# Early MLP units with a bank of their own for the third product, transposes at given places in PE's queue, two more pairs of split tiles, other banks for the first merge product

## The chip, the cores and the metric

The kernel runs on one core of one Trainium2 chip. A core has TensorE (PE in the profile; its weight loads are the row PEld), VectorE (DVE), ScalarE (ACT), GpSimd (POOL) and the queue SP, which here issues all DMAs. SBUF is the working memory; PSUM, eight banks of 128 x 512 float32, takes the results of PE. The metric is the device time of one execution in microseconds; less is better.

## The reference

One layer of a decoder trunk on x of 1024 tokens by 1024 channels, float32.

```python
h = rms_norm(x, norm_mix_pre)
proj = h @ w_in                       # q, k, v, z, ... of two mixers, two merge gates
y_a = gdn_branch(...)                 # gated DeltaNet, 4 heads
y_b = gla_branch(...)                 # gated linear attention, 4 heads
merged = sigmoid(gate_a) * (y_a @ w_out_a) + sigmoid(gate_b) * (y_b @ w_out_b)
x = x + rms_norm(merged @ w_o, norm_mix_post)
h = rms_norm(x, norm_mlp_pre)
u = square(relu(h @ w_mlp_up))        # 1024 -> 4096
x = x + rms_norm(u @ w_mlp_down, norm_mlp_post)
```

## The kernel before

**Precision and PE's work.** Each float32 product is made of three matmuls of a rounded format: an operand is split into a high part (cast by ACT) and the rest (subtraction by DVE). `split` makes such a pair in the pool `wsp`, tags `wh` and `wl`, three buffers each; `mm3` (line 256) issues hi*hi, hi*lo, lo*hi into one PSUM bank. A full matmul here is 128 x 128 weights by 512 columns.

**Queues.** The program is traced in the order of the code. A scheduler then gives each engine a fixed order: of what it takes to be ready at a modelled time, what comes first in the code goes first; `tc.high_priority(offset=...)` moves instructions forward (splits by `HP` = 2000 places, evictions of banks by `HPM` = 1500 or `HPE` = 2000). On the chip every engine then works its queue strictly in order and waits on semaphores. A tile of a tag with n buffers waits until a tile before it has had its last reader.

**PSUM.** The pool `psg` has four banks (`gbank()`, tile g), `psm` one bank each for the tags t, l, r, o (`mbank`, tiles mt, ml, mr, mo).

**Stages in order of time.** Input norm, projection and the two mixers; the merge; W_o with its norm and residual; MLP up; MLP down. The change touches the middle three:

1. *Merge* (lines 1002 to 1036). `load_o` loads and splits the outputs of the two mixers (`oaH/oaL`, `obH/obL`) through two `oraw` buffers. Gate groups 6 and 7 are computed: each a product into four g banks, a tanh of each bank into a tile `sg` (two buffers) and a store. Then, for c = 0 to 3, `ya` = four k tiles of branch A into four g banks (48 matmuls), `yb` = eight k tiles of branch B into four g banks (96 matmuls); DVE multiplies them with the gates and adds.

2. *W_o and norm* (lines 1100 to 1156). For each half u of the tokens: for two column halves c, sixteen steps in all, PE multiplies the merged activations of four token tiles (i = 0 to 3, one g bank each) by one k tile of w_o, twelve matmuls a step. The banks of each c are evicted into `m` (four tiles of that tag). Then for each token tile: the norm, the residual with a reloaded x (`xt`), the store of `d_x1`, the second norm by `stt(m, xt, rs, wpre2, ...)`, and a *turn*: eight PE transposes of `m` into the banks t and l, evicted into blocks. For u = 0 these are X11 and X21 (and their splits R11, R21); for u = 1, X12 and X22, and the sums that a Strassen-like scheme of seven products needs: T1, T2, R22, and X11, X21 rewritten. The X blocks are tiles of the tag `wu` of the pool `z`, which has four buffers. In the code each turn stands right behind its token tile's norm, ahead of the next half's products.

3. *MLP up.* A unit n (of 16) makes two blocks of 128 hidden channels (n and 16 + n), for both token halves, by seven products P1 to P7 of twelve matmuls each. For the first eight units (`NE` = 8), P1 and P2, which need only the first half of the tokens, run ahead (lines 1158 to 1180, "the P1/P2 loop", sixteen products in pairs of units), and their results go to DRAM (`d_p`, `d_u[0]`). `prep(n)` loads the weights of a unit (tag `wu`) and makes their sums (`ss`) on DVE. T3 and T4 are split from X22 and X21 behind the loop. Then, in a loop over n, an early unit (n < 8) runs P6 into bank A (r or o in turn), P5 into a g bank C, P7 added to A, P3 added to C, P4 added to A; each result is read out of A between the products and P1's saved result `p1` is added on DVE. A late unit runs P6, P5, P7, then P1 of the next unit, P4, P2 of the next unit, P3. `product` (line 1228) splits the operand in `wsp` and issues the twelve matmuls. `u_sums` makes the sums for the down projection and stores them; in the late units `down_sums` prepares sums of the down weights.

The lines of the products of a unit, before:

```python
s_P6(n); prep(n + 2); s_P5(n); s_P7(n)
# n >= 8: down_sums; and if a late unit follows: s_P1(n + 1), s_P4(n), s_P2(n + 1), s_P3(n)
# otherwise: s_P3(n); s_P4(n)
u_sums(n)
```

Of the kernel before, what the change touches and what calls it, by code (L numbers as in the profile page):

```python
# [7 lines left out]
F32 = mybir.dt.float32  # L8
# [3 lines left out]
ALU = mybir.AluOpType  # L12
# [11 lines left out]
TAU = 16.0  # L24
DFF = 4096
NE = 8
HP = 2000
HPX = 600
HPE = 2000
# [103 lines left out]
def kernel(  # L133
# [855 lines left out]
    with tc.tile_pool(name="mp", bufs=1, reuse_waits="tile") as mp:  # L989
        def load_o(src, n, nm):  # L990
            hi = mp.tile([P, n, S], F32R, name=nm + "H")
            lo = mp.tile([P, n, S], F32R, name=nm + "L")
            for k in range(n):
                for u in range(2):
                    us = slice(u * 512, u * 512 + 512)
                    raw = mp.tile([P, 512], F32, tag="oraw", name="oraw", bufs=2)
                    SP.dma_start(out=raw, in_=src[k, :, us])
                    with tc.high_priority(offset=HP):
                        A.copy(out=hi[:, k, us], in_=raw)
                        tt(lo[:, k, us], raw, hi[:, k, us].bitcast(F32), ALU.subtract)  # L1000
            return hi, lo
        oaH, oaL = load_o(d_oa, 4, "oa")
        obH, obL = load_o(d_ob, 8, "ob")
        run(gate_groups([int(c) for c in GTAIL.split()]))
        hp.release()
        bot = tc.alloc_tile_pool(name="bot", bufs=4, side="right", reuse_waits="tile")

        def big():
            return bot.tile([P, 8, 512], F32R, tag="big", name="big")

        mg_ = [(big(), big()) for _ in range(2)]
        for c in range(4):
            def sl(w):
                return lambda s: [w[:, 2 * s:2 * s + 2, c * 256:c * 256 + 256]]
            ya = gemm_fm(sl(woa), 4, oaH, oaL)
            ga = {}
            for b in range(2):
                for u in range(2):
                    sg = mp.tile([P, 512], F32, tag="sa", name="sa", bufs=4)
                    SP.dma_start(out=sg, in_=d_sig[c * 2 + b, :, u * 512:u * 512 + 512])  # L1020
                    with tc.high_priority(offset=HPE):
                        tt(sg, ya[b][u], sg, ALU.mult)
                    ga[b, u] = sg
            yb = gemm_fm(sl(wob), 8, obH, obL)
            for b in range(2):
                for u in range(2):
                    us = slice(u * 512, u * 512 + 512)
                    sg = mp.tile([P, 512], F32, tag="sb", name="sb", bufs=2)
                    SP.dma_start(out=sg, in_=d_sig[8 + c * 2 + b, :, us])
                    with tc.high_priority(offset=HPE):  # L1030
                        tt(sg, yb[b][u], sg, ALU.mult)
                    mg = ga[b, u]
                    with tc.high_priority(offset=HPM):
                        tt(mg, mg, sg, ALU.add)
                    A.copy(out=mg_[u][0][:, c * 2 + b, :], in_=mg)
                    tt(mg_[u][1][:, c * 2 + b, :], mg, mg_[u][0][:, c * 2 + b, :].bitcast(F32), ALU.subtract)
# [52 lines left out]
    with tc.tile_pool(name="op", bufs=1, reuse_waits="tile") as op:  # L1089
# [7 lines left out]
            tt(blk[:, kl, cs], src, blk[:, ks, cs].bitcast(F32), ALU.subtract)  # L1097

        k4 = slice(0, 4)
        for u in range(2):  # L1100
            ms, s2s = [], []
            for i in range(4):
# [2 lines left out]
            for c in range(2):  # L1105
                banks = [gbank() for _ in range(4)]
                cs = slice(c * 512, c * 512 + 512)
                for kt in range(KT):
                    hi, lo = load_slab512(wov[:, kt, cs], wsp, "w")
                    for i in range(4):  # L1110
                        il = slice(i * P, i * P + P)
                        mm3(banks[i], mg_[u][0][:, kt, il], mg_[u][1][:, kt, il], hi, lo, kt == 0, kt == KT - 1)
                with tc.high_priority(offset=HPE):
                    for i in range(4):
                        jk = op.tile([P, 512], F32, tag="jk", name="jk", bufs=1)
                        act(jk, banks[i], AF.Square, accum_out=s2s[i][:, c:c + 1])
                        tt(ms[i][:, cs], banks[i], wpost[:, cs], ALU.mult)
            if u == 1:
                T2, T1 = big(), big()
            for i in range(4):  # L1120
                t = u * 4 + i
                tsl = slice(t * P, t * P + P)
                rs = op.tile([P, 1], F32, tag="rs", name="rs", bufs=3)
                tt(rs, s2s[i][:, 0:1], s2s[i][:, 1:2], ALU.add, eng=G)
                rsqrt(rs, rs, 1.0 / D, EPS)
                m = ms[i]
                xt = z.tile([P, D], F32, tag="ss", name="xt", bufs=2)
                SP.dma_start(out=xt, in_=x2[tsl, :])
                stt(xt, m, rs, xt, ALU.mult, ALU.add)
                SP.dma_start(out=d_x1[tsl, :], in_=xt)  # L1130
                rs = op.tile([P, 1], F32, tag="rs", name="rs", bufs=3)
                act(m, xt, AF.Square, accum_out=rs)
                rsqrt(rs, rs, 1.0 / D, EPS)
                stt(m, xt, rs, wpre2, ALU.mult, ALU.mult)
                il = slice(i * P, i * P + P)
                pv = []
                for g in range(2):
                    pt = mbank("tl"[g])
                    for k in range(4):
                        T.transpose(out=pt[:, k * P:(k + 1) * P], in_=m[:, (g * 4 + k) * P:(g * 4 + k + 1) * P],  # L1140
                                    identity=ident)
                    pv.append(pt.rearrange("p (k c) -> p k c", c=P))
                if u == 0:
                    for g, n in enumerate(("11", "21")):
                        A.copy(out=X[n][:, :, il], in_=pv[g])
                        hilo(R[n], k4, il, X[n][:, :, il])
                else:
                    x11, x21, x12, x22 = (X[n][:, :, il] for n in ("11", "21", "12", "22"))
                    A.copy(out=x12, in_=pv[0])
                    tt(x22, pv[1], x12, ALU.subtract)  # L1150
                    hilo(R["22"], k4, il, pv[1])
                    tt(x12, x12, x11, ALU.subtract)
                    tt(x11, x22, x11, ALU.add)
                    hilo(T2, k4, il, x11)
                    hilo(T1, k4, il, x12)
                    tt(x21, x21, x11, ALU.subtract)

        for n in range(0, NE, 2):
            pair = range(n, n + 2)
            bank = {}  # L1160
            for p, k0, blk in (("P1", 0, R["11"]), ("P2", 4, R["21"])):
                for m in pair:
# [6 lines left out]
                    for k in range(4):  # L1169
                        mm3(bank[m], hi[:, k, :], lo[:, k, :], blk[:, k, :], blk[:, 4 + k, :],  # L1170
                            p == "P1" and k == 0, k == 3, p == "P2")
                    e = op.tile([P, 512], F32, tag="e", name="e", bufs=3)
                    with tc.high_priority(offset=HPM):
                        if p == "P1":
# [49 lines left out]
    with tc.tile_pool(name="ml", bufs=1, reuse_waits="tile") as ml:  # L1224
        RT = dict(P1=R["11"], P2=R["21"], P3=R["22"], P4=T4, P5=T1, P6=T2, P7=T3)
        reserve(ml, (("ev", 512, 10), ("us", 512, 6)))

        def product(n, p, ps, first):
            hi, lo = split(un[n][p], [P, 4, P], wsp, "w")
            for k in range(4):  # L1230
                mm3(ps, hi[:, k, :], lo[:, k, :], RT[p][:, k, :], RT[p][:, 4 + k, :], first and k == 0, k == 3, not first)

# [24 lines left out]
        def store(b, n, t):  # L1257
            SP.dma_start(out=d_u[b][:, n, :], in_=t)  # L1258

        def from_A(n, out):  # L1260
            if n < NE:
                tt(out, un[n]["A"], un[n]["p1"], ALU.add)
            else:
                A.copy(out=out, in_=un[n]["A"])

        def s_P1(n):
            x = un[n]
            x["A"] = mbank("ro"[n % 2])
# [14 lines left out]

        def s_P6(n):
            x = un[n]
            if n < NE:
                x["A"] = mbank("ro"[n % 2])
            product(n, "P6", x["A"], n < NE)
            x["c12"] = ev("c12")
            with tc.high_priority(offset=HPM):  # L1290
                from_A(n, x["c12"])

        def s_P5(n):
            x = un[n]
# [3 lines left out]
        def s_P7(n):  # L1298
# [1 line left out]
            product(n, "P7", x["A"], False)  # L1300
            x["c22"] = ev("c22")
            with tc.high_priority(offset=HPM):
                from_A(n, x["c22"])
                tt(x["c22"], x["C"], x["c22"], ALU.add)
            relu2(x["c22"], x["c22"])
            store(2, n, x["c22"])
# [1 line left out]
        def s_P4(n):  # L1308
# [1 line left out]
            product(n, "P4", x["A"], False)  # L1310
            x["c21"] = ev("c21")
            with tc.high_priority(offset=HPM):
                if n < NE:
                    from_A(n, x["c21"])
                    act(x["c21"], x["c21"], AF.Relu)
                else:
                    act(x["c21"], x["A"], AF.Relu)
            act(x["c21"], x["c21"], AF.Square)
            store(1, n, x["c21"])

        def s_P3(n):
            x = un[n]
            product(n, "P3", x["C"], False)
            with tc.high_priority(offset=HPM):
                tt(x["c12"], x["C"], x["c12"], ALU.add)
            relu2(x["c12"], x["c12"])

        def u_sums(n):
# [14 lines left out]
        for n in range(NU):  # L1343
            if n + 1 < NE:
                again(n + 1)
            s_P6(n)
            if n + 2 < NU:
                prep(n + 2)
# [1 line left out]
            s_P7(n)  # L1350
            if n >= NU // 2:
                down_sums(2 * n - NU)
            if NE <= n + 1 < NU:
                s_P1(n + 1)
                s_P4(n)
                s_P2(n + 1)
# [136 lines left out]
```

## Time and profile before

| | |
|---|---|
| median of 3 runs | 1718.45 us (1717.08 to 1719.82) |
| the profiled execution | 1717.46 us, of which the span is 1715.8 us |
| granted TensorE clock, mean | 0.994 |
| PE busy | 1659.6 us (97%), 9174 matmuls |
| DVE, ACT, POOL busy | 987.4, 769.1, 135.5 us |
| P1/P2 loop | from 1069.40 to 1120.09 us: 50.69 us, PE busy 47.97 |
| early units | from 1120.09 to 1235.98 us: 115.89 us, PE busy 108.74 |
| late units, first down product | from 1235.98 to 1413.60 us: 177.62 us, PE busy 175.46 |

A row of the profile in order of time reads: start in us from the span's start, duration in us, engine, line of the code, operation, output tile <- input tiles, shapes, how many in a row, and in brackets the idle time before it and what ended it. A line of a helper (67 is the matmul, 71 the transpose, 165 the two-operand DVE pass, 236 the cast of a split) stands for all its callers, so the tile names tell where an instruction belongs. Matmuls overlap: in a full stream one begins every 0.23 us, though its row says 0.39. A row of the waits reads: engine, tile and line <- engine, tile and line waited for: total us, times, longest.

### The profile page before, as it was taken

How to read it: one execution, taken by the hardware profiler on the slowest of the kernel's cores; microseconds unless marked ns; L12 is line 12 of the kernel's file. 1: busy time of each engine (PE TensorE's matmuls, PEld its weight loads, DVE VectorE, ACT ScalarE, POOL GpSimd, SP SyncE). 2: the span in 40 equal slices, each digit the busy share in tenths (PEclk: the TensorE clock that was granted, in tenths of full speed). 3: DMA queues.
4: the chain of work that ended last, by engine and by line, in shares of the span. 5: the costliest groups of instructions: out<-in, count | busy, mean ns of one | idle time of the engine just before them, and what ended most of it. 6: DMA issues, size and time to landing. Idle time of an engine off the chain costs nothing. (4 is left out here: it accounts for less than half of the span.)

```text
span 1715.8 us, 24483 instructions
## 1 busy us (share of the span) xinstructions
PE 1659.6 (97%) x9174; PEld 1402.4 (82%) x9174; DVE 987.4 (58%) x1678; ACT 769.1 (45%) x1576; POOL 135.5 (8%) x222
## 2 busy tenths in 40 slices
PE   7999999999999999999999999989999999999997
PEld 6888778878898998998788887777787778888886
DVE  5677565872544436543444455967776665564764
ACT  5456545643533235433421245744455555443442
POOL 2010111111101000101100011100000000000021
PEclk9999999999999999999999999999999999999999
DMA  5222213322211211123633344766578798776763
GB/s 166 56 72 75 83 38 91 91 62 68 76 44 44 62 50 50 37 63 126 218 117 112 122 163 150 244 223 221 179 259 279 239 327 304 257 261 224 245 226 136
DMA packets 186405, 251.39 MB, mean 147 GB/s; under 512 B 23351, under 2 KB 108430, under 8 KB 186286
## 3 DMA queue, kind: packets, MB, share of 16 engines
q1 hardware_dynamic: 186286, 249.83, 45.3%
q8 instruction: 72, 1.18, 0.3%
q14 instruction: 47, 0.39, 0.1%
HBM read 185.79 MB, written 63.98 MB: 146 GB/s over the span
## 5 line engine op out<-in xcount | busy, mean ns | idle before, releaser
L165 DVE TENSOR_TENSOR wl<-w,wh 128x512 fp32r<-128x512 f32 x181 | 125.7, 694 | 231.7 <-ACT wh L236 229.8
L67 PE MATMUL g<-hT,wh 128*128 128x512 f32 (+1 forms) x600 | 239.3, 399 | 1.5 <-DVE gr L174 0.9
L67 PE MATMUL g<-hL,wh 128*128 128x512 f32 (+1 forms) x600 | 232.9, 388 | 0.0
L67 PE MATMUL g<-hT,wl 128*128 128x512 f32 (+1 forms) x600 | 232.1, 387 | 0.0
L236 ACT CAST wh<-w 128x512 fp32r<-128x512 f32 x184 | 113.9, 619 | 212.8 <-PE g L67 194.4
L67 PE MATMUL g<-wh,hT 128*128 128x256 f32 x640 | 185.6, 290 | 0.0
L67 PE MATMUL g<-wh,hL 128*128 128x256 f32 x640 | 182.1, 285 | 0.0
L67 PE MATMUL g<-wl,hT 128*128 128x256 f32 x640 | 182.0, 284 | 0.0
L67 PE MATMUL g<-big 128*128 128x512 f32 x768 | 176.7, 392 | 2.4 <-ACT big L1219 2.4
L67 PEld LDWEIGHTS g<-big 128*128 128x128 f32 x768 | 145.2, 189 | 33.1 <-ACT big L1219 2.8
L165 DVE TENSOR_TENSOR big<-ru,big 128x1024 fp32r<-128x1024 f32 x53 | 64.9, 1224 | 115.9 <-ACT big L1219 115.5
L67 PEld LDWEIGHTS g<-hT,wh 128*128 128x128 f32 x600 | 113.6, 190 | 21.9 <-ACT sg L177 1.3
L67 PEld LDWEIGHTS g<-hT,wl 128*128 128x128 f32 x600 | 113.5, 189 | 21.6 <-DVE wl L165 0.2
L67 PEld LDWEIGHTS g<-hL,wh 128*128 128x128 f32 x600 | 113.9, 190 | 18.7 <-issue 1.0
L1219 ACT CAST big<-ru 128x1024 fp32r<-128x1024 f32 x53 | 55.8, 1053 | 154.8 <-PE g L67 57.7
L67 PEld LDWEIGHTS g<-wh,hT 128*128 128x128 f32 x640 | 123.1, 192 | 1.4 <-issue 1.0
L67 PEld LDWEIGHTS g<-wl,hT 128*128 128x128 f32 x640 | 123.2, 193 | 1.2 <-issue 1.0
L67 PEld LDWEIGHTS g<-wh,hL 128*128 128x128 f32 x640 | 123.2, 193 | 0.1
L177 ACT ACTIVATE c<-c 128x512 f32<-128x512 f32 x104 | 64.9, 631 | 49.6 <-DVE c L165 46.8
L67 PE MATMUL g<-wh,big 128*128 128x512 f32 x256 | 80.4, 392 | 0.0
L67 PE MATMUL mr<-big,wh 128*128 128x512 f32 x192 | 61.2, 400 | 6.1 <-DVE c L165 3.3
L165 DVE TENSOR_TENSOR big<-rv,big 128x1024 fp32r<-128x1024 f32 x53 | 64.5, 1218 | 0.1
(418 smaller groups left out, 3394.7 us busy)
## 6 DMA issues: line engine op xcount, KB each, us to landing
ru<-d_u SPq DMA_DIRECT2D x53, 512.0 KB, 4.5
w<-in_w_in_dram SPq DMA_DIRECT2D x80, 256.0 KB, 2.7
rv<-in_w_mlp_down_dram SPq DMA_DIRECT2D x37, 512.0 KB, 5.3
wu<-in_w_mlp_up_dram SPq DMA_DIRECT2D x32, 512.0 KB, 5.3
d_u<-c SPq DMA_DIRECT2D x56, 256.0 KB, 3.7
d_u<-us SPq DMA_DIRECT2D x48, 256.0 KB, 2.5
us<-in_w_mlp_down_dram SPq DMA_DIRECT2D x48, 256.0 KB, 4.2
xt<-in_x_dram SPq DMA_DIRECT2D x16, 512.0 KB, 5.4
```

Source lines behind the costliest of these rows:

```text
L67: return self.eng.matmul(out, lhsT, rhs, start=start, stop=stop, skip_group_check=more)
L165: (eng or V).tensor_tensor(out=out, in0=a, in1=b, op=op)
L177: A.activation(out=out, in_=a, func=func, **kw)
L236: A.copy(out=hi, in_=raw)
L1219: A.copy(out=s4[:, i], in_=raw)
```

## The change

Four edits, in the order of the program:

- The first `ya` (c = 0) of the merge goes to the banks r, o, l, t instead of the four g banks.
- The turns leave their place behind the norms and become a function. `TURNS` gives their places: for the first token half, after the steps 2, 5, 6 and 9 of the sixteen steps of the second half's W_o product; for the second half, after the products 3, 6, 10 and 12 (counted from 0) of the sixteen of the P1/P2 loop.
- `product` puts the split pairs of the products 1 and 3 of every five into the pool `wraw` (four buffers, no longer used at that stage) instead of `wsp`, in early and late units.
- The early units run as `early(n)`: P6 into A; P7 into a g bank d of its own, with no add on PE; P5 into a g bank c; P4 added to d; P3 added to c. The saved `p1` is added once, to P6's result, and that sum is added to d's contents on DVE. For the last early unit P1 and P2 of unit 8 stand between. Late units keep their order.

```diff
+TURNS = (2, 5, 6, 9), (3, 6, 10, 12)
...
-            ya = gemm_fm(sl(woa), 4, oaH, oaL)
+            ya = gemm_fm(sl(woa), 4, oaH, oaL, banks=[[mbank("r"), mbank("o")], [mbank("l"), mbank("t")]] if c == 0 else None)
...
+        def turn(u, i):
+            m = msu[u][i]
...
+            if u == 0:
+                for g, n in enumerate(("11", "21")):
+                    A.copy(out=X[n][:, :, il], in_=pv[g])
+                    hilo(R[n], k4, il, X[n][:, :, il])
+            else:
+                x11, x21, x12, x22 = (X[n][:, :, il] for n in ("11", "21", "12", "22"))
+                A.copy(out=x12, in_=pv[0])
+                tt(x22, pv[1], x12, ALU.subtract)
+                hilo(R["22"], k4, il, pv[1])
+                tt(x12, x12, x11, ALU.subtract)
+                tt(x11, x22, x11, ALU.add)
+                hilo(T2, k4, il, x11)
+                hilo(T1, k4, il, x12)
+                tt(x21, x21, x11, ALU.subtract)
...
                         mm3(banks[i], mg_[u][0][:, kt, il], mg_[u][1][:, kt, il], hi, lo, kt == 0, kt == KT - 1)
+                    if u and c * KT + kt in TURNS[0]:
+                        turn(0, TURNS[0].index(c * KT + kt))
...
+                    step = 2 * n + (2 if p == "P2" else 0) + m - n
+                    if step in TURNS[1]:
+                        turn(1, TURNS[1].index(step))
...
         def product(n, p, ps, first):
-            hi, lo = split(un[n][p], [P, 4, P], wsp, "w")
+            if turns[0] % 5 in (1, 3):
+                hi, lo = (wraw.tile([P, 4, P], F32R, tag="w", name="w" + x) for x in "hl")
+                with tc.high_priority(offset=HP):
+                    A.copy(out=hi, in_=un[n][p])
+                    tt(lo, un[n][p], hi.bitcast(F32), ALU.subtract)
+            else:
+                hi, lo = split(un[n][p], [P, 4, P], wsp, "w")
+            turns[0] += 1
...
+        def early(n):
+            x = un[n]
+            a, c, d = mbank("ro"[n % 2]), gbank(), gbank()
+            x["c12"], x["c22"], x["c21"] = ev("c12"), ev("c22"), ev("c21")
+            product(n, "P6", a, True)
+            with tc.high_priority(offset=HPM):
+                tt(x["c12"], a, x["p1"], ALU.add)
+            product(n, "P7", d, True)
+            with tc.high_priority(offset=HPM):
+                tt(x["c22"], d, x["c12"], ALU.add)
+            if n + 2 < NU:
+                prep(n + 2)
+            product(n, "P5", c, True)
+            with tc.high_priority(offset=HPM):
+                tt(x["c22"], c, x["c22"], ALU.add)
+            product(n, "P4", d, False)
+            with tc.high_priority(offset=HPM):
+                tt(x["c21"], d, x["c12"], ALU.add)
+            relu2(x["c22"], x["c22"])
+            store(2, n, x["c22"])
+            if n + 1 == NE:
+                s_P1(n + 1)
+            product(n, "P3", c, False)
+            with tc.high_priority(offset=HPM):
+                tt(x["c12"], c, x["c12"], ALU.add)
+            relu2(x["c21"], x["c21"])
+            store(1, n, x["c21"])
+            if n + 1 == NE:
+                s_P2(n + 1)
+            relu2(x["c12"], x["c12"])
...
+            if n < NE:
+                early(n)
+                u_sums(n)
+                continue
```

More of the change, by code (lines that the diff above doesn't have):

```diff
@@ L1099 @@
         k4 = slice(0, 4)
+        msu = []
+        def turn(u, i):
+            m = msu[u][i]
+            il = slice(i * P, i * P + P)
+            pv = []
+            for g in range(2):
+                pt = mbank("tl"[g])
+                for k in range(4):
+                    T.transpose(out=pt[:, k * P:(k + 1) * P], in_=m[:, (g * 4 + k) * P:(g * 4 + k + 1) * P],
+                                identity=ident)
+                pv.append(pt.rearrange("p (k c) -> p k c", c=P))
+            if u == 0:
[12 more added lines that the diff above has]
+                tt(x21, x21, x11, ALU.subtract)
         for u in range(2):
@@ L1134 @@
                 stt(m, xt, rs, wpre2, ALU.mult, ALU.mult)
[L1135 to L1156, printed above, removed]
+            msu.append(ms)
         for n in range(0, NE, 2):
@@ L1226 @@
         reserve(ml, (("ev", 512, 10), ("us", 512, 6)))
+        turns = [0]
         def product(n, p, ps, first):
-            hi, lo = split(un[n][p], [P, 4, P], wsp, "w")
+            if turns[0] % 5 in (1, 3):
[6 more added lines that the diff above has]
+            turns[0] += 1
             for k in range(4):
@@ L1258, in store @@
             SP.dma_start(out=d_u[b][:, n, :], in_=t)
[L1260 to L1264, printed above, removed]
         def s_P1(n):
@@ L1285, in s_P6 @@
             x = un[n]
-            if n < NE:
-                x["A"] = mbank("ro"[n % 2])
-            product(n, "P6", x["A"], n < NE)
+            product(n, "P6", x["A"], False)
             x["c12"] = ev("c12")
             with tc.high_priority(offset=HPM):
-                from_A(n, x["c12"])
+                A.copy(out=x["c12"], in_=x["A"])
         def s_P5(n):
@@ L1302, in s_P7 @@
             with tc.high_priority(offset=HPM):
-                from_A(n, x["c22"])
+                A.copy(out=x["c22"], in_=x["A"])
                 tt(x["c22"], x["C"], x["c22"], ALU.add)
@@ L1312, in s_P4 @@
             with tc.high_priority(offset=HPM):
[L1313 to L1317, printed above, removed]
+                act(x["c21"], x["A"], AF.Relu)
             act(x["c21"], x["c21"], AF.Square)
@@ L1352 @@
                 down_sums(2 * n - NU)
-            if NE <= n + 1 < NU:
+            if n + 1 < NU:
                 s_P1(n + 1)
```

## The prediction

> **What bounds the kernel now.** I read the page's first lines, then the waits of PE, then PE's rows in order of time around the four stages that the change touches.
>
> ```profile
> span 1715.8 us, 24483 instructions
> PE 1659.6 (97%) x9174; PEld 1402.4 (82%) x9174; DVE 987.4 (58%) x1678; ACT 769.1 (45%) x1576; POOL 135.5 (8%) x222
> ```
>
> PE is busy for 97% of the span, and the change removes none of its matmuls. So only PE's waits, and the slow matmuls that follow long waits, can be won. The waits of PE name them:
>
> ```profile
> PE g L67 <- ACT sg L177: 2.8, 2, 2.2
> PE mr L67 <- DVE c L165: 3.3, 1, 3.3
> PE mo L67 <- ACT wh L236: 1.9, 4, 0.5
> PE mr L67 <- ACT wh L236: 1.4, 3, 0.5
> PE mr L67 <- ACT c L1264: 1.1, 1, 1.1
> PE mo L67 <- ACT c L1264: 1.0, 1, 1.0
> ```
>
> Columns: total us, times, longest. To these come the waits of the x1 transposes, asked for in two windows: the second W_o half (us 1018 to 1067) and the P1/P2 loop (1068 to 1121).
>
> ```profile
> PE mt L71 <- DVE m L174: 2.7, 3, 1.5
> PE mt L71 <- DVE m L174: 2.7, 4, 0.8
> ```
>
> The profiled execution took 1717.46 us, 1.66 over its span and 0.99 under the median of 1718.45; I sum against the execution and take the same saving off the median.
>
> **Part A: other banks for the merge.** Rows of PE where the merge begins, and of ACT:
>
> ```profile
> 839.51 0.39 PE L67 MATMUL g<-hT,wl 128*128 128x512 f32 x1
> 840.03 0.50 PE L67 MATMUL g<-oaH,wh 128*128 128x512 f32 x1
> 842.66 0.39 PE L67 MATMUL g<-oaH,wl 128*128 128x512 f32 x1
> 845.26 0.50 PE L67 MATMUL g<-oaH,wh 128*128 128x512 f32 x1 [2.21 <-ACT sg L177]
> 855.17 0.39 PE L67 MATMUL g<-obH,wh 128*128 128x512 f32 x1
> 844.61 0.60 ACT L177 ACTIVATE sg<-g 128x512 f32<-128x512 f32 x1 [1.45 <-DMA d_sig<-sg]
> 846.22 0.60 ACT L177 ACTIVATE sg<-g 128x512 f32<-128x512 f32 x1
> ```
>
> The first product of `ya` needs the four g banks that gate group 7 still holds; their tanh waits for a store that frees an `sg` tile. A normal matmul follows the last after 0.23. From 839.51 to 840.03 are 0.29 too many, from 842.66 to 845.26 2.37 too many. From 845.26 to 855.17 lie the 36 remaining matmuls of `ya`: 9.91 us instead of 36 x 0.2275 = 8.19, so the slow start after the wait costs 1.72. In banks r, o, l, t nothing is left to wait for: their last users, the GLA transposes, stand ahead of gate groups 6 and 7 in PE's queue. Sum 4.4. What is late next: `yb` then starts at 839.74 + 48 x 0.2275 = 850.7 instead of 855.17; its g banks are free at 846.8 (last tanh above), so the banks do not hold it. The loads of `obH` go on beside it, some 4 us nearer to their use; if that cover were gone one load would show, about 2 us. I take 4.4, ends 2.4 and 4.4.
>
> **Part B: transposes of the first half amid the second W_o GEMM.** A turn has eight transposes. Its cost on PE and the worst wait:
>
> ```profile
> 1034.85 0.63 PE L71 MATMUL mt<-ident,m 128*128 128x128 f32 x4 [1.51 <-DVE m L174]
> 1035.67 0.47 PE L67 MATMUL g<-wh,big 128*128 128x512 f32 x1
> ```
>
> Eight transposes take 0.82 in the queue, before and after alike. The turn at 1034.85 is the third of four; that GEMM ended at 1069.40 (a row of part C), and sixteen steps of 2.73, four turns and the waits before that, at about 1019, it began. The new places are after steps 2, 5, 6 and 9, so its third turn comes at 1019 + 7 x 2.73 + 2 x 0.82 = 1039.7, 4.9 after its input is there. The norms that make the input are not moved, a turn issues no DMA, and neither POOL's nor SP's queue is passed. The waits of 2.7 go, and 3 x 0.16 of overlap that a matmul has with the one before it: 3.2. One thing is new: `m` has four tiles, and the second half's fourth eviction (after step 7) now needs the tile that the turn after step 9 reads. Bank 3 of step 8 is held by it; other banks' matmuls, 9 x 0.23 = 2.05 of step 10, can run meanwhile, against transposes, one DVE pass of 0.69 and its queue. I charge 0.5: 2.7, ends 1.2 and 3.2.
>
> **Part C: transposes of the second half among the P1/P2 units.** Here the move has a price. The loop has sixteen products; the first early unit follows it.
>
> ```profile
> wu<-in_w_mlp_up_dram SPq DMA_DIRECT2D x32, 512.0 KB, 5.3
> 1069.40 0.61 PE L67 MATMUL mr<-R,wh 128*128 128x512 f32 x2
> 1095.01 0.63 PE L71 MATMUL mt<-ident,m 128*128 128x128 f32 x4 [0.84 <-DVE m L174]
> 1101.31 0.68 DVE L165 TENSOR_TENSOR big<-wu,big 128x512 fp32r<-128x512 f32 x1
> 1105.66 0.68 DVE L165 TENSOR_TENSOR big<-wu,big 128x512 fp32r<-128x512 f32 x1
> 1106.40 1.01 SPq L1072 DMA_DIRECT2D wu<-in_w_mlp_up_dram  x2
> 1113.29 0.69 DVE L165 TENSOR_TENSOR ss<-wu 128x512 f32<-128x512 f32 x1
> 1114.79 0.62 ACT L236 CAST wh<-ss 128x512 fp32r<-128x512 f32 x1 [0.81 <-DVE ss L165]
> 1120.09 0.62 PE L67 MATMUL mr<-big,wh 128*128 128x512 f32 x2
> 1128.97 1.05 PE L67 MATMUL mr<-big,wh 128*128 128x512 f32 x2 [3.28 <-DVE c L165]
> 1133.16 0.39 PE L67 MATMUL mr<-big,wl 128*128 128x512 f32 x1
> 1128.14 0.69 DVE L165 TENSOR_TENSOR c<-mr,p 128x512 f32<-128x512 f32 x1 [1.29 <-DMA p<-d_p]
> ```
>
> The X blocks fill all four `wu` tiles. `prep(0)`, which loads the first early unit's weights into such a tile, is issued at 1106.40, right behind the end (1106.34) of the fourth turn's last T1 pass. Before, there was slack: weights split at 1115.4, used at 1120.09.
>
> Now count from 1069.40 = 0. Before, P6(0) begins at 50.7, and the third product (P7, behind the 3.28 wait and slow matmuls) ends at 1133.16 + 0.23, which is 64.0. After: sixteen products and four turns without waits end at 16 x 2.727 + 4 x 0.82 = 46.9. The fourth turn starts after step 12, at 13 x 2.727 + 3 x 0.82 = 37.9. From a turn's first transpose to its last T1 pass, the turn at 1095.01 took until 1101.99: 6.98. So the tile is free at 44.9. The second load is issued 0.5 later and lands 5.3 after that: 50.7. Two DVE passes and the cast take 1114.79 + 0.62 - 1113.29 = 2.12: P6(0) starts at about 52.9, a new wait of 6.0 where there was none. P7 and P5 follow at once, for the own bank frees P7 from the P6 eviction. That eviction waits for a DMA of `p` behind the loop; it had landed by 1128.14, 8.0 after the loop's end, which is now 54.9, ahead of P6's end at 57.3. With a slow start of 1.7 the three products end at 52.9 + 3 x 2.727 + 1.7 = 62.8. Gain 1.2. Ends: a chain 4 us longer makes it -2.8; no wait at all makes it 64.0 - 46.9 - 8.2 = 8.9.
>
> The slow start is from rows: idle of 2.21 and 3.28 was followed by matmuls at about half speed, idle of 1.51 was not. [...]
>
> **Part D: the early units (own bank, five pairs of split tiles).** The first two rows begin P6(1) and P6(7); the next two begin successive products in the late part; the last two are P6(1)'s last matmul and its eviction on DVE.
>
> ```profile
> 1134.03 0.73 PE L67 MATMUL mo<-big,wh 128*128 128x512 f32 x2 [0.48 <-ACT wh L236]
> 1222.25 0.73 PE L67 MATMUL mo<-big,wh 128*128 128x512 f32 x2 [0.48 <-ACT wh L236]
> 1235.98 0.62 PE L67 MATMUL mr<-R,wh 128*128 128x512 f32 x2
> 1238.70 0.62 PE L67 MATMUL mo<-big,wh 128*128 128x512 f32 x2
> 1142.12 0.39 PE L67 MATMUL mo<-big,wl 128*128 128x512 f32 x1
> 1144.50 0.68 DVE L165 TENSOR_TENSOR c<-mo,p 128x512 f32<-128x512 f32 x1
> ```
>
> Six units take 88.22, 14.70 each; five products of 2.72 are 13.60. So 1.10 per unit is lost: the wait for the split of P6 (0.48, a split pair that comes free too late), the wait of P7 for the P6 eviction (0.10 idle), the rest overlap and slower first matmuls. 6 x 1.10, and 0.64 ahead of P6(1): 7.2 to be had. Two more pairs let a split run two products (5.4 us) earlier, and P7 in a bank of its own waits for no eviction. What takes their place: P4 adds to that bank and needs the eviction of P7, with P5's 2.73 as cover. The eviction must wait for its turn on DVE: the one at 1144.50 came 2.2 after its product's last matmul had passed (1142.12 + 0.23). 2.2 + 0.7 is just over the cover, so some units will wait a few tenths. DVE and ACT get no more passes than now. I take 5.5, ends 0 and 7.2.
>
> **Part E: late units.** They have only the two further pairs. Rows of ACT, then of PE:
>
> ```profile
> 1328.98 0.60 ACT L236 CAST wh<-wu 128x512 fp32r<-128x512 f32 x1
> 1329.49 0.58 ACT L1264 COPY c<-mr 128x512 f32<-128x512 f32 x1
> 1330.12 0.73 PE L67 MATMUL mr<-big,wh 128*128 128x512 f32 x2 [1.13 <-ACT c L1264]
> ```
>
> A split ahead of an eviction in ACT's queue makes P7 wait, twice so far, 2.1 in all. More pairs may remove this or make more of it: 0, ends -3 and +2.
>
> **Sum.** 4.4 + 2.7 + 1.2 + 5.5 + 0 = 13.8. The execution becomes 1717.46 - 13.8 = 1703.7, the median 1718.45 - 13.8 = 1704.7.
>
> **The rivals.**
> 1. `prep(0)` is in time after all. For it: before, its split stood ready 4.7 before PE came. Against: the fourth turn moves from 27.9 to 37.9 on the clock of part C. Part C then gives 8.9: 1704.7 - 7.7 = 1697.0. In between, a wait of some 3 leaves 1704.7 - 3 = 1701.7 by the rows. [...]
> 2. The own bank only swaps the wait: P4 waits for the P7 eviction as P7 waited for P6's, and the split is still behind other ACT work. For it: the 2.2 lag on DVE above. Against: ACT is idle for about half the time. Part D gives 0: 1710.2.
> 3. The scheduler keeps to its own order, so that transposes go ahead of their input as now. Then B and the loop's 2.7 stay lost, but the fourth turn is early and `prep(0)` in time: about 1704.7 + 2.7 + 2.7 - 7.7 = 1702.4, within the forecast.
> 4. Slower: splits overtake evictions. Five pairs put more splits ahead of evictions in ACT's and DVE's fixed order, and the wait of 1.1 that two of the late units show comes at P7 and at P4 of all sixteen units: 32 x 1.1 = 35, giving 1704.7 + 5.5 + 35 = 1745. It decides for slower from about 13 such waits on top of the present ones. For it: the row pair at 1328.98. Against: six of the eight late units have none, and a ring of pairs runs ahead only once.
>
> **How the numbers follow.** Forecast with its spread (and rival 3) 0.57; rival 1 with its halfway case 0.18 (0.12 and 0.06); rival 2 0.19; rival 4 0.06. The predicted time is the forecast's, 1704.7. The range runs from rival 1's 1697 to rival 2 with a somewhat longer chain in C, 1712: it leaves out rival 4 and the tails of the parts' ends, about 2 in 10. A measurement of this kernel can tell 0.2%, 3.4 us, from no change. Faster by more: forecast, rival 1 and most of rival 2, 0.88. Within: part D at 0 with C or E at their low ends, 0.06. Slower: rival 4, 0.06.
>
> **What would show it.** A: no idle before the thirteenth matmul of the first `ya`, no slow matmuls there. B and C: no PE wait for `m`; instead a PE wait of 4 to 7 us before the first early unit, ended by a split of `ss`, its load issued behind T1's last pass. D: the early period near 13.8, no wait for `wh`. The prediction is wrong if the wait before the first unit is missing or above 10, or if PE waits for `c` once in most units.

## The result and the profile after

The changed kernel takes 1701.66 us, median of 5 runs (1699.28 to 1702.45); the kernel before, on the same chip, 1719.36 us (1717.08 to 1720.12). The ratio is 0.9897, interval [0.9883, 0.9912]: some 18 us, or 1.0%, faster, and 3.0 us under the predicted 1704.7. The profiled execution took 1699.28 us.

The first lines of the page of the changed kernel (busy time, share of the span, instructions):

```profile
span 1697.5 us, 24475 instructions
PE 1653.0 (97%) x9174; PEld 1403.0 (83%) x9174; DVE 987.2 (58%) x1678; ACT 771.5 (45%) x1576; POOL 135.9 (8%) x222
```

PE has the same 9174 matmuls and is 6.6 us less busy, and the span is 18.2 shorter, so 11.6 of the gain is idle time. What PE still waits for from the merge to the last early unit, in the view of waits for us 837 to 1281 (total, times, longest); it lists three rows in all:

```profile
PE mr L68 <- ACT wh L237: 4.7, 1, 4.7
PE ml L72 <- DVE R L166: 2.4, 1, 2.4
PE g L68 <- DVE m L166: 0.2, 1, 0.2
```

The waits for `sg` in the merge, the seven for `wh`, the one of 3.3 for `c`, and those of the transposes for `m` are gone. Two new ones stand in their place, both in the P1/P2 loop or at its end. Three stretches, first before, then after: the first `ya`, the loop, and the first three products of the early units (the view of windows: length, busy time of each engine, then PEclk, the granted clock):

```profile
840.03:855.17 15.14, 12.93 (x48) 10.21 (x49) 6.95 (x12) 6.82 (x13) 2.67 (x4) 0.89 0.72 232
1069.40:1120.09 50.69, 47.97 (x225) 38.99 (x224) 45.86 (x64) 38.42 (x71) 10.46 (x18) 1.00 0.78 248
1120.09:1134.03 13.94, 10.18 (x38) 7.64 (x36) 7.66 (x13) 3.58 (x6) 0.00 (x0) 0.88 0.92 286
```
```profile
837.97:848.85 10.88, 10.88 (x50) 9.01 (x48) 3.84 (x6) 4.75 (x9) 2.58 (x4) 1.00 0.75 239
1060.67:1116.85 56.18, 49.09 (x225) 40.29 (x223) 44.51 (x61) 39.05 (x72) 10.90 (x18) 0.95 0.65 212
1116.85:1127.62 10.77, 10.77 (x36) 8.31 (x37) 9.71 (x16) 3.31 (x7) 0.00 (x0) 0.77 1.12 357
```

The first `ya` now runs without idle at 0.227 us a matmul (10.88 / 48) and a granted clock of 1.00. The loop became 5.5 longer, and its clock and that of the products behind it show slow matmuls (0.95 and 0.77; in a second profile of the same kernel the loop is 4.0 longer and has 0.99, see below). The whole span by stages, each length the difference between the starts of two matmuls in PE's rows:

| stage | before | after | gain |
|---|---|---|---|
| start to the first `ya` | 840.03 | 837.97 | 2.06 |
| A: first `ya` | 15.14 | 10.88 | 4.26 |
| `yb` and the rest of the merge | 119.68 | 119.84 | -0.16 |
| B: both W_o halves | 94.55 | 91.99 | 2.56 |
| C: P1/P2 loop to the end of the third early product | 64.63 | 66.95 | -2.32 |
| D: the next 35 products | 102.17 | 95.43 | 6.74 |
| E: late units | 160.70 | 157.58 | 3.1 |
| last up product to the end | 318.85 | 316.91 | 1.9 |
| sum | 1715.75 | 1697.54 | 18.2 |

From the first `ya` to the last up product 14.2 of it are gained. D is exactly 35 x 2.727: early units lose nothing any more.

Where C went. PE's rows of the second moved turn, then of the first early unit:

```profile
1083.63 0.63 PE L72 MATMUL ml<-ident,m 128*128 128x128 f32 x4 [2.42 <-DVE R L166]
1084.01 0.99 PE L68 MATMUL mo<-R,wh 128*128 128x512 f32 x2
1086.51 1.05 PE L68 MATMUL mo<-R,wh 128*128 128x512 f32 x2
1116.85 1.22 PE L68 MATMUL mr<-big,wh 128*128 128x512 f32 x2 [4.67 <-ACT wh L237]
1118.60 1.05 PE L68 MATMUL mr<-big,wh 128*128 128x512 f32 x2
```

Both waits are followed by matmul pairs of about 1.05 us where 0.61 or 0.62 is normal in this trace; the granted clock is 0.83 in the ten microseconds behind the first and 0.77 in the three products behind the second. DVE's rows behind the first wait:

```profile
1080.99 1.29 DVE L175 SCALAR_TENSOR_TENSOR m<-xt,rs,wpre 128x1024 f32<-128x1024 f32 x1 [0.71 <-POOL rs L186]
1082.20 0.68 DVE L166 TENSOR_TENSOR wl<-w,wh 128x512 fp32r<-128x512 f32 x1
1082.80 0.68 DVE L166 TENSOR_TENSOR R<-ml,R 128x512 fp32r<-128x512 f32 x1
```

The last reader of bank l in the first turn is the split of R22. In DVE's fixed order it stands behind a norm pass that waits for POOL (1080.99), so the bank comes free at 1083.5, and the second turn, which comes three products after the first, waits for it. The chain behind the second wait, in rows of DVE, SP and ACT:

```profile
1107.12 2.42 DVE L166 TENSOR_TENSOR big<-wu,big 128x1024 fp32r<-128x1024 f32 x3
1109.02 1.01 SPq L1073 DMA_DIRECT2D wu<-in_w_mlp_up_dram  x2
1114.73 0.69 DVE L166 TENSOR_TENSOR ss<-wu 128x512 f32<-128x512 f32 x1 [0.58 <-DMA wu<-in_w_mlp_up_dram]
1116.18 1.14 ACT L237 CAST wh<-ss 128x512 fp32r<-128x512 f32 x2 [2.33 <-DVE ss L166]
```

The first row stands for three passes, of which the second ends at 1108.93. The loads of `prep(0)` are issued right behind it (1109.02 and 1109.44), so this is the T1 pass that frees their tile. The sum `ss` waits for the loads, and the first cast of the last row ends at 1116.80, 0.05 before PE goes on.

### The profile page after: what moved, and what is told of

The parts are those of the page before. It is cut to its first block, busy times and chain, and to the rows that moved or that the text cites. A ratio compares the mean times of both kernels' runs of the same rounds, so it can differ in the third digit from the quotient of the medians.

```text
span 1697.5 us, 24475 instructions
## 1 busy us (share of the span) xinstructions
PE 1653.0 (97%) x9174; PEld 1403.0 (83%) x9174; DVE 987.2 (58%) x1678; ACT 771.5 (45%) x1576; POOL 135.9 (8%) x222
## 4 chain that ended last, share of the span: by engine, by line
PE 82%; DVE 7%; DMA 4%; ACT 4%; issue 2%; POOL 1%; SPq 0%; DVEq 0%; ACTq 0%; POOLq 0%
PE g L68 58%; PE mr L68 8%; PE mo L68 7%; PE ml L68 4%; PE mt L68 3%; DMA gb<-d_g 2%; DVE Xt L166 1%; PE mt L72 1%; DVE Xi L548 1%; DVE wl L166 1%; ACT E L178 1%; DMA oraw<-d_oa 1%; ACT wh L237 0%; DMA rv<-in_w_mlp_down_dram 0%; ACT Zp L604 0%
## 5 line engine op out<-in xcount | busy, mean ns | idle before, releaser
L68 PE MATMUL g<-big,wh 128*128 128x512 f32 x256 | 78.8, 389 | 0.0
```

Of the source, the lines that this page charges most:

```text
L68: return self.eng.matmul(out, lhsT, rhs, start=start, stop=stop, skip_group_check=more)
```

## The experiments

What had to be told apart: which edit brings which gain; whether the wait before the first early unit is set by the fourth turn's release of a `wu` tile (theory X) or by something that does not move with that turn; whether the early units gain by the own bank (O) or by the further pairs; and whether the remaining waits of the transposes are for DVE's `m` (D) or for the banks t and l. In each, all else is as in the changed kernel. Ratios are to the kernel before, timed on the same chip.

### Merge in the g banks again

```diff
-ya = gemm_fm(sl(woa), 4, oaH, oaL, banks=[[mbank("r"), mbank("o")], [mbank("l"), mbank("t")]] if c == 0 else None)
+ya = gemm_fm(sl(woa), 4, oaH, oaL)
```

> The changed kernel with the first ya back in the four g banks. Theory: the banks alone carry part A. The wait of 2.2 us on the tanh of gate group 7 and the slow matmuls behind it come back: ya of c = 0 takes 15.1 us instead of 10.9, the kernel is 4 to 4.5 us slower than the changed one (1705.7 to 1706.2). Rival: the obH loads, which the earlier yb comes nearer to, or a later wait take it back, and the time differs by under 1 us.

Measured: 1705.8 us, ratio 0.9934 [0.991, 0.9958]. The first `ya` takes 14.42 instead of 10.88. PE's rows there:

```profile
840.07 0.50 PE L68 MATMUL g<-oaH,wh 128*128 128x512 f32 x1 [0.39 <-ACT sg L178]
843.05 0.50 PE L68 MATMUL g<-oaH,wh 128*128 128x512 f32 x1 [1.33 <-ACT sg L178]
845.64 0.50 PE L68 MATMUL g<-oaH,wh 128*128 128x512 f32 x1 [0.93 <-ACT sg L178]
```

The waits for `sg` are back, in three pieces. The banks carry stage A: 3.5 us here. It is less than the 4.26 against before: the waits came in three pieces, and none was followed by slow matmuls. The granted clock of the stage was 1.00, against 0.89 before:

```profile
838.16:852.58 14.42, 11.77 (x50) 8.78 (x48) 5.88 (x9) 6.46 (x11) 2.33 (x4) 1.00 0.65 212
```

### All turns back behind their norms

```diff
-                    if u and c * KT + kt in TURNS[0]:
-                        turn(0, TURNS[0].index(c * KT + kt))
...
+                turn(u, i)
...
-                    if step in TURNS[1]:
-                        turn(1, TURNS[1].index(step))
```

> The changed kernel with all turns back behind their norms. Theory: the place of the second half's turns costs more than it saves, because the fourth turn frees the tile that the first early unit's weights are loaded into, and the bank of its own already removes the 3.28 us wait of P7. Then the W_o half has its 2.7 us of waits again (2.6 slower), the P1/P2 loop takes 50.7 as before, but P6, P7, P5 of unit 0 follow with no wait: they end about 59 us after the loop's start instead of 66.9. Net 4 to 6 us faster than the changed kernel, 1696 to 1698. Rival (the reckoning of the prediction's part C, moves together worth some 4 us): slower than the changed kernel by 3 to 5 us, about 1705.5.

Measured: 1699.09 us, 0.9898 [0.9876, 0.992]. B is 94.45 (2.46 worse than with the move), C 58.82 (8.1 better), D 96.90 (1.5 worse). By stages the moves together cost 4.2 against the profile shown above (2.9 against a second one, see the next experiment); the ratios alone can't tell it, and the time is above the 1696 to 1698 that was expected. In C the loop's two new waits are gone and the four small ones for `m` are back.

### Only the second half's turns back

```diff
+                if u:
+                    turn(u, i)
...
-                    if step in TURNS[1]:
-                        turn(1, TURNS[1].index(step))
```

> The changed kernel with only the second half's turns back behind their norms; those of the first half stay at their given places. Theory: the two moves are independent. The W_o half stays at 92.0 us (94.45 with both undone), loop start to third product is 58.8 as with both undone: 7 to 8 us faster than the changed kernel, 1693.5 to 1695. Rival: the first half's later turns delay the second half's norms or evictions and the loop starts with a wait; over 61 us.

Measured: 1695.01 us, 0.9863 [0.9845, 0.988]. B keeps its gain (91.87), C is 58.84. The waits of PE from the loop to the end of the early units, and the first matmuls of the first unit:

```profile
PE mt L72 <- DVE m L175: 2.7, 4, 0.8
PE g L68 <- DVE c L166: 1.4, 1, 1.4
```
```profile
1110.64 0.39 PE L68 MATMUL mo<-R,wl 128*128 128x512 f32 x1
1110.87 0.61 PE L68 MATMUL mr<-big,wh 128*128 128x512 f32 x2
1113.59 0.61 PE L68 MATMUL g<-big,wh 128*128 128x512 f32 x2
```

P6(0) starts without idle or slow start, and P7, in its g bank, follows 2.72 later: the three products take 8.16. So the 3.28 wait of before does not need the moved turns to go; the own bank is enough. (A wait of 1.36 for an eviction, which needs the reloaded P1 result `p`, comes one product later: D is 97.09.) Against the profile shown above, the move of the second half's turns costs 66.95 - 58.84 = 8.1 in C and gives back 1.66 in D. The same kernel was timed again, beside the changed kernel itself:

> The changed kernel itself, beside its variants on the same chip. All theories: loop start to third product 66.9 us, early units 95.4 without a wait; about 0.990 of the kernel before.

> Only the second half's turns back behind their norms, once more. Theory: loop start to third product 58.8 us, 8.1 less than the changed kernel; the first early unit's wait for p gives 1.6 back; 6 to 7 us faster than the changed kernel on the same chip, about 0.986 of the kernel before. Rival: the earlier verdict was chip noise, under 3 us.

The changed kernel: 1700.25 us (1699.08 to 1701.32), 0.9894 [0.9875, 0.9913]. With the second half's turns back: 1695.3 us (1694.32 to 1697.17), 0.987 [0.9848, 0.9892]. The two intervals against before overlap, but none of the five runs of the one reaches those of the other: 5.0 us between the medians, less than the 6 to 7 expected. The profiles of these two say why. In the second profile of the changed kernel C is 65.61 and not 66.95: the wait for bank l is there too (2.52), but no slow matmuls follow it. Against 58.81 with the turns back, the move then costs 6.8 in C and gives back 1.9 in D (95.43 against 97.31), 4.9 in all. So some 1.3 of the 8.1 belong to the one execution, not to the change.

### The fourth turn two products later

```diff
-TURNS = (2, 5, 6, 9), (3, 6, 10, 12)
+TURNS = (2, 5, 6, 9), (3, 6, 10, 14)
```

> The changed kernel with the last of the second half's turns after product 14 of the P1/P2 loop instead of 12. Theory X (the fourth turn frees the tile for the first early unit's weights): everything behind that turn moves by two products, 5.45 us, so PE's wait before P6(0), 4.67 in the changed kernel, becomes 9.5 to 10.5, still ended by the split of ss, and the stretch from the loop's start to the third product of unit 0 becomes 72 to 73 us (66.95). Rival Y (something behind the loop's end sets that wait: the order of the T3 and T4 passes on DVE, the load's own place in SP's queue): the wait stays at 4 to 6.

Measured: 1704.68 us, a single time. The row of PE's waits, then rows of DVE and SP:

```profile
PE mr L68 <- ACT wh L237: 11.0, 1, 11.0
```
```profile
1110.47 2.42 DVE L166 TENSOR_TENSOR big<-wu,big 128x1024 fp32r<-128x1024 f32 x3
1112.99 1.03 SPq L1073 DMA_DIRECT2D wu<-in_w_mlp_up_dram  x2
1119.24 0.69 DVE L166 TENSOR_TENSOR ss<-wu 128x512 f32<-128x512 f32 x1 [2.27 <-DMA wu<-in_w_mlp_up_dram]
```

The wait grew from 4.67 to 11.03, more than the two products (5.45) and than the 9.5 to 10.5 expected. C grew from 66.95 to 72.40. That this is exactly 5.45 is chance, since here no slow matmuls follow the wait for bank l (2.91); against the second profile of the changed kernel, which has none either, it grew by 6.8. The loads are again issued right behind a T1 pass (1112.89 and 1112.99), and `ss` waits for them. The excess of 0.9 lies in that chain: the first load is issued 6.42 after the fourth turn's start instead of 6.04, and `ss` begins 5.80 after the second load's issue instead of 5.29. What holds the first unit moves with the fourth turn: X is shown.

### Other banks for the second half's transposes, and earlier places

```diff
-                pt = mbank("tl"[g])
+                pt = gbank() if u else mbank("tl"[g])
```

> The changed kernel with the second half's transposes in two g banks, idle in that loop, instead of t and l. Theory: the wait of 2.42 us inside the second turn (bank l still read by the R22 split, which stands behind the norms on DVE) goes, and the slow matmuls behind it, 4.3 us in all; the wait before P6(0) grows by nothing or a little, since the fourth turn comes that much earlier too. Loop start to third product 62 to 63.5 us; 3.5 to 4.5 us faster than the changed kernel. Rival: the fourth turn's chain on DVE is what PE waits for in the end and does not move, so that the wait before P6(0) takes the 4.3 back: 66 to 67 us, no faster.

Measured: 1695.97 us, 0.9872 [0.9856, 0.9887]. All waits of PE from the loop to the end of the early units:

```profile
PE mr L68 <- ACT wh L237: 4.7, 1, 4.7
PE mr L68 <- ACT e L1187: 0.4, 1, 0.4
PE mo L68 <- ACT e L178: 0.2, 1, 0.2
```

The wait of 2.42 for bank l is gone, which shows what it was; the wait before P6(0) did not change (4.71). C is 64.32, where 62 to 63.5 was expected: 2.6 better than in the profile above, and 1.3 better than in the second one, whose wait had no slow matmuls behind it. The full 4.3 is not reached, in part because two small waits for P1/P2 evictions come up (0.56) and the first three products take 11.20 instead of 10.77. Next, with these banks, the last turns earlier:

```diff
-TURNS = (2, 5, 6, 9), (3, 6, 10, 12)
+TURNS = (2, 5, 6, 9), (3, 6, 8, 10)
```

> The second half's transposes in g banks and their places 3, 6, 8, 10 instead of 3, 6, 10, 12. Theory X: the fourth turn is two products (5.45 us) earlier, so the tile for the first early unit's weights is free 5.45 earlier and the wait before P6(0) goes to 0 to 1, with no slow matmuls behind it: loop start to third product 55 to 57.5 us, 9 to 11 us faster than the changed kernel, some 1691 to 1693. Rival Y: the wait stays at 4 or more: 61 us or more.

Measured: 1697.72 us, 0.9878 [0.9863, 0.9894]; C is 61.57, where 55 to 57.5 was expected: a miss. The loop and the first three products in the view of windows:

```profile
1059.54:1110.81 51.27, 48.22 (x226) 38.96 (x224) 43.83 (x61) 37.55 (x70) 10.62 (x18) 1.00 0.69 226
1110.81:1121.10 10.29, 9.98 (x36) 7.87 (x37) 9.22 (x16) 4.42 (x9) 0.00 (x0) 0.83 1.07 331
```

The fourth turn came 6.1 earlier after the loop's start than in the kernel above (33.08 instead of 39.20), but the first load of `prep(0)` was issued only 2.6 earlier (42.63 instead of 45.24): the chain from the transposes to that load grew from 6.04 to 9.55. The second load followed 1.53 behind the first, with a store between them, instead of 0.43, and `ss` began only 1.8 earlier. DVE is busy for 43.83 of these 51.27 us, in a fixed order, so a turn that comes earlier finds other passes ahead of its own. That DVE's queue made the chain longer is read from the profile, not tried by itself. A wait of 1.72 stayed, and even that was followed by slow matmuls. Earlier again:

```diff
-TURNS = (2, 5, 6, 9), (3, 6, 10, 12)
+TURNS = (2, 5, 6, 9), (3, 5, 7, 9)
```

> Transposes of the second half in g banks after the products 3, 5, 7 and 9. Theory X alone: the fourth turn is one more product (2.7 us) earlier than with 3, 6, 8, 10, the wait before P6(0) of 1.72 goes and with it the slow matmuls, 57 to 58 us from loop start to third product. Theory D (by then DVE's queue holds the chain, not the turn's place): the fourth turn's passes take longer again, the wait stays at 0.5 to 2 and the stretch at 60 to 61.5.

Measured: 1695.91 us, 0.9868 [0.9848, 0.9889]. The wait before P6(0) is gone, as X says, and C is 58.01. But in PE's waits of that stretch stands now, beside three of 0.8, 0.7 and 0.3,

```profile
PE g L68 <- DVE c L166: 2.1, 1, 2.1
```

This is the wait for the reloaded `p` at the fourth product; with a slow start behind it (granted clock 0.83 in the ten microseconds from 1123.97), D is 99.45 instead of 95.43. C and D together: 157.5, against 162.4 and 161.0 in the two profiles of the changed kernel and 156.1 with the turns behind the norms. The tile's lateness had covered the next late thing.

### Turns back, in g banks

```diff
-                pt = mbank("tl"[g])
+                pt = gbank() if u else mbank("tl"[g])
...
+                if u:
+                    turn(u, i)
...
-                    if step in TURNS[1]:
-                        turn(1, TURNS[1].index(step))
```

> As the run before, with these transposes in two g banks. Theory D (DVE sets the loop's length, 46 to 51 of its 51 us are DVE passes): the transposes wait for m, not for a bank, so the four waits of 2.7 us stay, 58.5 to 59.1 us. Rival B (banks): some of these waits are the banks', and the loop gets 1 to 3 us shorter.

Measured: 1695.06 us, 0.9866 [0.9847, 0.9885]; C is 58.65. The waits of the transposes stay, with another tile's name:

```profile
PE g L72 <- DVE m L175: 2.5, 4, 0.8
```

So at the old places the norms on DVE hold the transposes, not the banks (D). This version and the one with the turns back in t and l are the fastest found, 0.24 apart, which can't be told. Nor can they be told by time from two of the kernels with moved turns in g banks, less than 1 us slower (1695.97 and 1695.91); there only the stages C and D speak for the old places.

### Three pairs of split tiles instead of five

```diff
-            if turns[0] % 5 in (1, 3):
+            if False:
```

> The changed kernel with three split pairs for all products. Theory O (own bank): with the new order P6, P7, P5, P4, P3 the pair that P6 of the next unit takes was freed two products before, so the early period stays at 13.6 us and the kernel loses at most the 2 to 3 us of the late units, 1701.7 to 1704.5. Theory P (pairs): the wait of 0.48 for P6's split comes back in each early unit, the period is 14.1 to 14.4, and with the late units the kernel is 6 to 8 us slower, 1707.5 to 1709.5.

Measured: 1704.41 us, 0.993 [0.9906, 0.9953]. D stays at 95.43; E becomes 159.79. In the late units waits for evictions are back:

```profile
1317.36 0.74 PE L68 MATMUL mr<-big,wh 128*128 128x512 f32 x2 [0.27 <-ACT c L1304]
1337.11 0.73 PE L68 MATMUL mo<-big,wh 128*128 128x512 f32 x2 [0.38 <-ACT c L1304]
```

The early units do not need the two pairs; the late units gain 2.2 by them.

### Early units as before, with five pairs

```diff
-            if n < NE:
-                early(n)
-                u_sums(n)
-                continue
```

(and P6, P7 and P4 of these units in one bank, with `p1` added to each result, as before)

> The changed kernel with the early units as before (P7 added to P6's bank) and five split pairs. Theory O: the P7 wait for P6's eviction and the order that the scheduler makes of it stay; early period 14.2 to 14.7, and the first unit waits again for the DMA of p: 5 to 9 us slower than the changed kernel, 1707 to 1711. Theory P: early period 13.6 to 13.9, at most 3 us slower, 1702 to 1704.7. In the late units both expect no wait of 1.1 us for c if the pairs removed it.

Measured: 1707.75 us, 0.9944 [0.9924, 0.9963]. D is 101.45, E 157.56. Two of PE's rows:

```profile
1157.88 0.73 PE L68 MATMUL mr<-big,wh 128*128 128x512 f32 x2 [0.94 <-DVE c L166]
1161.67 0.72 PE L68 MATMUL mr<-big,wh 128*128 128x512 f32 x2 [0.78 <-DVE c L166]
```

With five pairs the waits for `wh` are gone, but a product now waits for the eviction of the one before it in its bank, and of the 6.74 only 0.7 is left. With the row of three pairs above: the own bank and its order carry D alone (the two, and the single addition of `p1`, were not tried apart), the pairs carry the late units (157.56 here against 160.70 before).

## Why the prediction was right

Time and direction were right, and the sum of the parts (13.8) was close to what those stages gave (14.2). That it was so close is in part luck: C fell short by 3.5, D and E brought 4.4 more than forecast, and the total hides it.

- **A, 4.4 for 4.26.** As worked out; the thirteenth matmul follows the twelfth as every other does:

```profile
840.46 0.39 PE L68 MATMUL mo<-oaH,wl 128*128 128x512 f32 x1
840.69 0.39 PE L68 MATMUL ml<-oaH,wh 128*128 128x512 f32 x1
```

  No idle, no slow start, and the g banks of `yb` held nothing up. Undone alone it costs 3.5.
- **B, 2.7 for 2.56.** The waits for `m` are gone but for one of 0.2, the price of the fourth `m` tile, charged at 0.5.
- **C, +1.2 for -2.3.** The chain was right in kind: the fourth turn moves, with it the tile, the load, the split, and PE waits for `ss` within the 4 to 7 given (4.67). With the g banks, where little else (0.56 in two waits) disturbed the loop, P6(0) began 53.12 after the loop's start; 52.9 was predicted. What failed is the step "sixteen products and four turns without waits": the second turn waited 2.42 for bank l, and the slow matmuls behind it cost about 1.6 more. The sum asked whether a turn's input `m` was ready and how late its last pass was, not who still reads the PSUM bank that the next turn writes. That put the fourth turn at 42.30 after the loop's start instead of 37.9 (at 40.81 in the second profile, where the wait had no slow matmuls behind it and C's gain is -1.0). Three smaller differences: P6(0) followed the fourth turn's start after 13.9 instead of 15.0, since the T1 pass that frees the tile ended 5.96 after that start and not 6.98, the slow start behind the wait cost 2.6 (10.77 instead of 8.16) instead of 1.7, and the stage before was 64.63, not 64.0. Together -4.4 + 1.1 - 0.9 + 0.6 = -3.6, which is the distance between +1.2 and -2.3 but for rounding.
- **C, what belonged to which edit.** The gain of the own bank for P7(0) stood in C beside the cost of the moved turns, and the positive balance hid that the move itself only costs. With the turns behind their norms C gains 5.8 (64.63 - 58.84), and the kernel comes to 1695.3, near rival 1's 1697.0: `prep(0)` is then in time, since the fourth turn stays early. The 1701.66 measured for the change itself is next to the 1701.7 of rival 1's halfway case, but by chance: that case needed a wait of some 3 and a better C.
- **D, 5.5 for 6.74.** The early period is 13.63 and no wait for `wh` is left. The eviction of P7, feared as a new wait of a few tenths for P4, never appears. The prediction credited pairs and bank together; the bank and its order do it alone.
- **E, 0 for +3.1.** The term was mis-sized. Both signs were argued for the pairs; the two waits of 2.1 behind a split are gone, and three pairs bring back waits for evictions and 2.2 of the 3.1. Where the other 0.9 comes from is open.
- **Outside the parts: 4.0.** 1.9 lie behind the last up product. There PE's wait for a cast of the down weights was 2.4 before and 1.6 after, in code that was not changed; a second profile of the changed kernel has 3.6, and that stretch took from 316.9 to 321.5 us over the changed kernel and its variants, with 318.85 before in the middle. So it is spread between executions. Of the 2.06 ahead of the first `ya` some 0.6 are shorter waits for `sg`, and other small waits of code that was not changed are 0.9 shorter in all (the rows of PE's waits up to us 830 sum to 26.6 before and 25.4 after, 0.3 of it for `sg`). The rest stays open: the thirteen profiles of the changed kernel and its variants reach `ya` between 836.7 and 838.8 us, the one of before at 840.03.
- **The rivals.** 2 (the wait only swaps) and 4 (splits overtake evictions) are excluded by D and E. 3 is excluded by the rows: the turns stand where `TURNS` puts them. In rival 4 the "about 13 such waits" fit the forecast's 1704.7 ((1718.45 - 1704.7) / 1.1 = 12.5), not its own start of 1710.2, from which 8 would do.

## What to carry to other kernels

When work is moved back in a queue to fill an engine, follow every buffer that it reads or writes to whoever wants it next, weight loads and PSUM banks of the next piece too: here one part of the change lost 5 of the 22 us that the others brought (1717.06 to 1695.3), because a tile and a bank came free too late for their next writers. An accumulation that must be read out in between is worth a bank of its own, with an order of products to match, where one is free: here 6.0 us over 35 products (101.45 against 95.43). More operand buffers didn't replace it. Where several late things are stacked, as the tile, the DVE queue and the reloaded `p` are here, taking one away shows the next, so time the parts of a change apart before keeping them all. And profile a kernel twice before giving a stage's difference of 1 or 2 us to a change.

## What was not expected of the hardware

In these profiles the length of an idle time of PE does not by itself decide whether slow matmuls follow, as the prediction's rows of 2.21, 3.28 and 1.51 let it appear. The wait of the second turn for bank l stands at the same place in six profiles, with the same work behind it. Its length does not go together with the time per matmul behind it (from the second matmul pair to the next matmul, halved) or with the granted clock of the ten microseconds after it:

| profile | wait, us | us per matmul behind it | granted clock after it |
|---|---|---|---|
| merge in the g banks | 2.09 | 0.43 | 0.83 |
| early units as before | 2.11 | 0.23 | 1.00 |
| the changed kernel | 2.42 | 0.43 | 0.83 |
| the changed kernel, second profile | 2.52 | 0.23 | 1.00 |
| three pairs | 2.90 | 0.43 | 0.83 |
| fourth turn two products later | 2.91 | 0.23 | 1.00 |

The windows of the third and the fourth row (PEclk, the granted clock, is the third column from the right):

```profile
1083.63:1093.63 10.00, 10.00 (x39) 8.18 (x40) 8.54 (x14) 6.32 (x12) 0.00 (x0) 0.83 0.49 157
```
```profile
1082.84:1092.84 10.00, 10.00 (x46) 8.35 (x47) 9.05 (x15) 7.43 (x14) 0.00 (x0) 1.00 0.61 194
```

In ten microseconds 39 matmuls were recorded in the one and 46 in the other. The clock records of the kernel before and of the changed kernel (first profile) show where the granted clock was 0.50, in us from the span's start:

| trace | stretches at 0.50 |
|---|---|
| before | 129.02 to 132.44, 845.82 to 849.24, 1129.13 to 1132.54, 1415.85 to 1419.26, from 1709.39 to the end |
| after | 128.54 to 131.95, 1084.27 to 1087.68, 1114.99 to 1121.82, from 1691.84 to the end |

Within each of these two traces the stretches start whole multiples of 3.413 us apart (845.82 - 129.02 = 716.80, which is 210 of them), and each takes one or two such steps, 3.41 or 6.83 (but for the last, at the end of the program). Laid on that grid, from us 20 on, seven waits of PE have 2.07 to 3.25 us in one step, and the step behind it is at 0.50: among them the waits of 2.21, 3.28 and 2.42, and the first 2.81 of the 4.67. Behind a step in which no wait has more than 1.56, none is at 0.50, the end of the program apart; the wait of 1.51 in the W_o half is cut by a boundary into 0.22 and 1.29. What sets the clock is not shown by this, since no run moved a wait against the grid. How much idle time is enough stays open too: of whole waits, 1.59 had no slow matmuls behind it (turns back; clock 1.00), 1.72 had (places 3, 6, 8, 10; 0.83), and 2.91 had none in the last row of the first table.

The loss behind a wait of 4.67 or 4.71 before P6(0) was 2.6 and 3.0 us: the first three products took 10.77 and 11.20 instead of 8.16.
